# Strassen's seven products in the down projection, with the residual stream kept token-major

## The chip, the cores and the metric

One core of one Trainium2 chip. The metric is the device time of one execution in microseconds (us); the times shown are medians of several runs. Everything is computed in float32 precision: an operand is held as two float32r parts, a high part and the remainder, and a product of two operands takes three matmuls on TensorE (`mm3`: high by high, high by low, low by high).

## What is computed

One layer of a decoder trunk for 512 tokens with 1024 channels. Cut to what the change touches:

```python
x = x + (g_a * y_a + g_b * y_b) @ w_out[i]                     # 1024 x 1024
h = rmsnorm(x, ffn_norm[i])
x = x + conv_ffn(h, w_up[i], conv_w[i], conv_b[i], w_down[i])   # 1024 -> 2 * 2816, causal conv of width 3,
                                                               # gelu(a) * b, 2816 -> 1024
gate = jax.nn.sigmoid(rmsnorm(x, ple_norm[i]) @ w_ple_gate[i])  # 1024 x 1024
x = x + gate * (p[i] @ w_ple[i])                               # 256 -> 1024
return rmsnorm(x, final_norm)
```

Ahead of it stand two mixers (an input projection to five outputs of 1024 channels, pooling, spatial gating, two branch projections); the change leaves their arithmetic as it was.

## The kernel before

The work runs in stages one behind the other: input projections, mixers, branch projections, output projection (`w_out`), up projection with the convolution, down projection, and the last stage (embedding gate, embedding, final norm, output).

**Layouts.** A tile holds 128 channels by 512 tokens (channel-major) or 128 tokens by 1024 channels (token-major). Contractions need their operand channel-major. The mixer's output `ga` is token-major; `turn` (L566) turns it by 32 TensorE transposes of 128x128. From there the residual `x` is channel-major until the last stage, where `turn_back` (L688) turns it into token-major tiles `xt`, again 32 transposes. The norm before the up projection is not applied to its input: its factor, a row over tokens, is made on TensorE (`Norm.token` L257, four matmuls of one column; `Norm.row` L263, two matmuls of 512 columns) while the first up projections run, and each of the 44 up outputs is multiplied by it on VectorE (L607).

**Weights.** `plan` queues each block of weights (128x1024, 512 KB). `take` hands out the next one and keeps two more ready; `prepare` loads up to four ahead on SP's DMA queue (L77), then cuts the block in two: ScalarE makes the high part `whi` (L64), VectorE the remainder `wlo` (L65). The cut parts stand in four pairs of buffers, so a block's cut waits until TensorE is through with the block four places ahead.

**Seven products.** Three of the input projections and the embedding gate use Strassen's scheme in Winograd's form (`seven`, L312): a product of two operands, each seen as 2 by 2 blocks, from seven block products in place of eight. The sums of activation blocks are made by `combine` (L284), the sums of weight blocks on VectorE (L101) or, for the embedding gate's first two, by an accumulating DMA on POOL's queue (L96). The partial results stand in two PSUM banks `seeded` that are copied out by ScalarE (L349, L352) before the next product adds to them.

**Down projection.** `down` (L628) accumulates 22 channel tiles into each of eight outputs, 128 channels by 512 tokens: 22 x 8 x 3 = 528 matmuls of 512 columns. The operands of the embedding gate (`operands`, L640) are made while the down projection still runs for three of the four pairs of channel tiles; the fourth is made behind it.

The order of instructions on each engine is set by the tile framework when the program is built, from the order in which the code is written and from dependencies; on the chip each engine then goes through its own list in that order.

Of the kernel before, what the change touches and what calls it, by code (L numbers as in the profile page):

```python
# [32 lines left out]


# [6 lines left out]
def trunk(ctx, tc, xT, pT, wsT, par, bsp, w_u0, w_u1, w_v, w_ga, w_gb, w_p, w_pl,  # L41
# [37 lines left out]

    def plan(src, cols=CW, **kw):  # L80
        got = []
        todo.append((lambda: got.append(load_raw(src)), lambda: parts(got[0], cols, **kw)))

    def plan_seven(w, summed=False, spare=()):

        raw = {}

        def unit(load_, dst, kk, add=None):  # L90
            def load():
                if load_:
                    name, *src = load_
                    t = raw[name, kk] = load_raw(w["abdc".index(src[0]), kk])
                    for z in src[1:]:
                        G.dma_start(t, w["abdc".index(z), kk], accum_op=ALU.add)  # L96

            def cut():
                t = raw[dst, kk]
                if add:  # L100
                    V.tensor_tensor(t, t, raw[add, kk], op=ALU.add)  # L101
                return parts(t, spare=dst in spare and not add)

            todo.append((load, cut))

        for args in ((("a", "a"), "a"), (("t", "b", "a"), "t"), (("c", "c"), "t", "c"), (("s", "b", "c"), "s"),
                     (("d", "d"), "t", "d"), (None, "d"), (None, "c")) if summed else (
                     (("a", "a"), "a"), (("b", "b"), "a", "b"), (("c", "c"), "a", "c"), (None, "b", "c"),
                     (("d", "d"), "a", "d"), (None, "d"), (None, "c")):
            for kk in range(2):  # L110
                unit(args[0], args[1], kk, *args[2:])
# [18 lines left out]
    plan_seven(w_v)  # L130
    plan_seven(w_ga)
    plan_seven(w_gb)
# [11 lines left out]
    for f in range(KD):  # L144
        plan(w_o[f].rearrange(flat))
    for i in range(2 * KF):
        plan(w_up[i].rearrange(flat))
    DK = [(k0, min(8, KF - k0)) for k0 in range(0, KF, 8)]
    ORDER = [f for k in range(HK) for f in (k, HK + k)]

    def plan_down(f, k0, n):
        plan(w_dn[f, :, k0:k0 + n, :].rearrange(flat), n * P)

    for f in ORDER[:-2]:
        for k0, n in DK:
            plan_down(f, k0, n)
    for k0, n in DK:
        for f in ORDER[-2:]:
            plan_down(f, k0, n)
    for k in range(2):  # L160
        plan(w_ple[k])
    plan_seven(w_g, summed=True, spare="c")
# [123 lines left out]
    def combine(k, s1, s2, E):  # L286

        d = work("d").rearrange("p (a t) -> p a t", a=2)
        e = work("e").rearrange("p (a t) -> p a t", a=2)
        E.tensor_tensor(d[:, 0], s1[:, H:], s2[:, H:], op=ALU.subtract)  # L290
        E.tensor_tensor(d[:, 1], d[:, 0], s1[:, :H], op=ALU.subtract)
        E.tensor_tensor(e[:, 0], s1[:, :H], s1[:, H:], op=ALU.subtract)
        E.tensor_tensor(e[:, 1], s2[:, :H], d[:, 1], op=ALU.add)
        o = []
        for src in (d, e):
            t = block("cmb", (2, 2, H), F32R)
            S.copy(t[:, :, 0], src)
            V.tensor_tensor(t[:, :, 1], src, t[:, :, 0].bitcast(F32), op=ALU.subtract)
            o.append(t)
        return o  # L300

    class Operand:


        def __init__(self, whole, cmb):
            self.whole, self.cmb = whole, cmb

        def get(self, c, k, j):

            if c in ("A11", "A12", "A22"):  # L310
                t, c0 = self.whole[k + (HK if c[2] == "2" else 0)], H if c[1] == "2" else 0
            else:  # L312
                i = ("D", "S2", "S3", "E").index(c)
                t, c0 = self.cmb[k][i // 2][:, i % 2], 0
            return act(t, slice(c0 + j * P, c0 + (j + 1) * P))

    def seven(op, drain, fill=(), tail=False):

        fill = list(fill)
        ahead = AHEAD + 2 if tail else AHEAD

        def step(o, c, w, kk, first):
            for j, c0, n, t in o:
                for k2 in range(2):
                    k = 2 * kk + k2
                    mm3(t, op.get(c, k, j), [z[:, c0:c0 + n] for z in wslice(w, k2, T)], first and k == 0, k == HK - 1,
                        skip_group_check=True)

        def product(o, c, first=False):
            for kk in range(2):
                step(o, c, take(ahead), kk, first)
                if fill:
                    fill.pop(0)()

        def whole(banks):
            return [(j, 0, T, t) for j, t in enumerate(banks)]

        a, b = whole([bank() for _ in range(2)]), whole(seeded)  # L340
        product(a, "A11", first=True)
        for j in range(2):
            S.copy(seeded[j], a[j][3])
        c = [(0, 0, T, bank())] + ([(1, 0, H, bank()[:, :H]), (1, H, H, bank()[:, :H])] if tail else [(1, 0, T, bank())])
        product(c, "D", first=True)
        product(b, "S2")
        u = [[work("u") for _ in range(2)] for _ in range(2)]
        for j in range(2):
            S.copy(u[0][j], seeded[j])  # L349
        product(b, "S3")  # L350
        for j in range(2):
            S.copy(u[1][j], seeded[j])  # L352

        def minus(p, z):
            j, c0, n, t = p
            o = z[j][:, c0:c0 + n]
            V.tensor_tensor(o, t, o, op=ALU.subtract)  # L357
            return o

        for p in c:  # L360
            minus(p, u[1])
        for j in range(2):
            drain(1, j, 1, u[1][j], 0)
        product(b, "A22")
        for j in range(2):
            drain(1, j, 0, seeded[j], 0)
        product(a, "A12")
        for j, _, _, t in a:
            drain(0, j, 0, t, 0)
        if not tail:  # L370
            product(c, "E")
            for p in c:
                drain(0, p[0], 1, minus(p, u[0]), 0)
        else:
            ws = [take(ahead) for _ in range(2)]
            for p in c:
                for kk in range(2):
                    step([p], "E", ws[kk], kk, False)
                drain(0, p[0], 1, minus(p, u[0]), p[1])
        for f in fill:  # L380
            f()
# [45 lines left out]
    cmb = []  # L427
# [4 lines left out]
    for f in range(KD):  # L432
# [4 lines left out]
        if f % 2:  # L437
            k = f // 2
            s = []
            for i in (k, HK + k):  # L440
                s.append(work("sx"))
                S.activation(s[-1], x[i], AF.Copy, scale=col(C_MIX, i))
            cmb.append(combine(k, *s, V))
    X = Operand(xg, cmb)
# [40 lines left out]
    def gate(op, fill=()):  # L485
# [8 lines left out]
        seven(op, drain, fill)  # L494
# [60 lines left out]
    x2.clear()  # L555
    x.clear()
    for k in range(KD):
        if k % 2 == 0:
            x2.append(block("x"))
        x.append(x2[-1][:, k % 2])  # L560
        later(x[k][:, :1], ga[0][:, 0, :1])
        nc.scalar.dma_start(x[k], xT[k])

    m = []

    def turn(fs):  # L566

        for f in fs:
            tp = bank()
            for b in range(NT):  # L570
                PE.transpose(tp[:, b * P:(b + 1) * P], ga[b][:, f // 4, f % 4 * P:(f % 4 + 1) * P], ident)  # L571
            m.append(split(tp))

    def residual(f, o, cg, nm=None):

        V.tensor_tensor(x[f], o, x[f], op=ALU.add)
        b = split(x[f], col(cg, f))
        if nm is not None:
            nm.add(x[f])
        return b  # L580
# [10 lines left out]
    for f in range(2):  # L591
        for k in range(HK, KD):
            mm3(seeded[f], wslice(c[f], k), act(m[k]), False, k == KD - 1)
        xg.append(residual(f, seeded[f], C_FFN, nm))
    for f in range(2, KD):
        xg.append(residual(f, proj8(m), C_FFN, nm))


    up_o = [proj8(xg)]
    r_tok = nm.token()  # L600
    up_o.append(proj8(xg))
    R = nm.row(r_tok)

    def conv(i):
        o = up_o[i] if i < len(up_o) else proj8(xg)
        z = work("up")
        V.tensor_tensor(z, o, R, op=ALU.mult)  # L607
        cc = work("cc")
# [38 lines left out]

    for f in ORDER[:-2]:
        down([f])
# [167 lines left out]
```

## Time and profile before

| | |
|---|---|
| median of 3 runs | 790.32 us (790.09 to 791.33) |
| the profiled execution | 790.46 us, of which the span in the trace is 788.8 us |
| TensorE (PE) busy | 775.5 us, 98% of the span |
| VectorE (DVE) busy | 524.5 us, 67% |
| ScalarE (ACT) busy | 362.7 us, 46% |
| GpSimd (POOL) busy | 31.2 us, 4% |
| moved by DMA | 86.68 MB |

Busy shares are means over stages with different limits. Matmuls overlap: one lasts 390 ns and the next starts 227 ns behind its start, so TensorE's work is counted in starts.

### The profile page before, as it was taken

Reading aid. Unit: us, or ns where it says so; the run is one execution under the profiler, and the core shown is the slowest. Engines: PE = TensorE matmul, PEld = TensorE weight load, DVE = VectorE, ACT = ScalarE, POOL = GpSimd, SP = SyncE. Lnnn points to the kernel's source line nnn. Section 1 sums busy time; section 2 is a strip of 40 time slices with the busy share of each in tenths; the row PEclk is TensorE's granted clock in tenths of the full one; section 3 lists DMA queues with packets and bytes.
Section 4 is the critical chain, followed back from the end, with each engine's and each line's share of the span. In section 5 each row is a group of like instructions: output and inputs, shape, how many; then the busy total and the mean of one; then the engine's idle time right before and its main releaser. Section 6 shows DMA issues by size and latency. Waiting matters only on the chain.

```text
span 788.8 us, 9104 instructions
## 1 busy us (share of the span) xinstructions
PE 775.5 (98%) x3502; PEld 643.5 (82%) x3502; DVE 524.5 (67%) x713; ACT 362.7 (46%) x499; POOL 31.2 (4%) x68
## 2 busy tenths in 40 slices
PE   9999999999999999999999999999999999999994
PEld 8888878888888888888888888888888888888883
DVE  7797898865576744665877777777776234355666
ACT  6576736582142321442644444444444223244974
POOL 0000200000112100000000000000000000000201
PEclk9999999999999999999999999999999999999998
DMA  9612225134031507515221121211216430137302
GB/s 351 267 54 81 80 81 187 53 108 161 27 133 57 211 11 282 210 58 187 81 81 53 54 80 56 80 54 53 81 52 224 138 101 0 47 134 236 84 1 107
DMA packets 26683, 86.68 MB, mean 110 GB/s; under 512 B 3088, under 2 KB 3216, under 8 KB 26640
## 3 DMA queue, kind: packets, MB, share of 16 engines
q1 hardware_dynamic: 23904, 79.70, 28.5%
q10 hardware_dynamic: 2160, 4.31, 1.6%
q0 software_dynamic: 576, 2.10, 1.5%
q8 instruction: 27, 0.44, 0.2%
q14 instruction: 16, 0.13, 0.0%
HBM read 84.00 MB, written 2.10 MB: 109 GB/s over the span
## 4 chain that ended last, share of the span: by engine, by line
PE 94%; DVE 3%; ACT 1%; issue 1%; POOL 0%; POOLq 0%; ACTq 0%; DVEq 0%
PE mm L166 26%; PE mm L167 26%; PE mm L168 25%; PE sd L167 5%; PE sd L166 5%; PE sd L168 5%; PE mm L475 1%; DVE raw L101 1%; PE wake L223 1%; DVE xt L724 0%; PE mm L571 0%; DVE wlo L65 0%; DVE ple L723 0%; ACT whi L64 0%; DVE u L357 0%
## 5 line engine op out<-in xcount | busy, mean ns | idle before, releaser
L64 ACT CAST whi<-raw 128x1024 fp32r<-128x1024 f32 (+2 forms) x165 | 171.1, 1039 | 253.1 <-PE mm L167 123.0
L65 DVE TENSOR_TENSOR wlo<-raw,whi 128x1024 fp32r<-128x1024 f32 (+1 forms) x172 | 203.1, 1185 | 116.3 <-ACT whi L64 114.8
L166 PE MATMUL mm<-blk,whi 128*128 128x512 f32 x704 | 274.0, 390 | 0.0
L167 PE MATMUL mm<-blk,whi 128*128 128x512 f32 x704 | 273.9, 389 | 0.0
L168 PE MATMUL mm<-blk,wlo 128*128 128x512 f32 x704 | 273.8, 389 | 0.0
L166 PEld LDWEIGHTS mm<-blk,whi 128*128 128x128 f32 x704 | 132.4, 188 | 28.0 <-ACT blk L201 0.3
L168 PEld LDWEIGHTS mm<-blk,wlo 128*128 128x128 f32 x704 | 132.1, 188 | 27.5
L167 PEld LDWEIGHTS mm<-blk,whi 128*128 128x128 f32 x704 | 132.2, 188 | 27.3
L166 PE MATMUL mm<-whi,blk 128*128 128x512 f32 x160 | 62.7, 392 | 0.0
L167 PE MATMUL mm<-wlo,blk 128*128 128x512 f32 x160 | 62.4, 390 | 0.0
L168 PE MATMUL mm<-whi,blk 128*128 128x512 f32 x160 | 62.3, 389 | 0.0
L607 DVE TENSOR_TENSOR up<-mm,R 128x512 f32<-128x512 f32 x44 | 30.2, 687 | 38.5 <-PE mm L168 38.5
L198 ACT CAST blk<-cc 128x512 fp32r<-128x512 f32 x22 | 13.7, 621 | 57.3 <-DVE cc L621 57.3
L609 ACT ACTIVATE cc<-up,pr 128x512 f32<-128x512 f32 x44 | 35.7, 813 | 1.8 <-DVE up L607 1.6
L166 PEld LDWEIGHTS mm<-whi,blk 128*128 128x128 f32 x160 | 30.0, 188 | 6.4 <-ACT mm L696 0.2
L168 PEld LDWEIGHTS mm<-whi,blk 128*128 128x128 f32 x160 | 30.0, 188 | 6.2
L167 PEld LDWEIGHTS mm<-wlo,blk 128*128 128x128 f32 x160 | 30.1, 188 | 6.0
L612 DVE SCALAR_TENSOR_TENSOR cc<-up,pr,cc 128x510 f32<-128x510 f32 x44 | 33.0, 749 | 1.5
L101 DVE TENSOR_TENSOR raw<-raw 128x1024 f32<-128x1024 f32 x28 | 33.8, 1228 | 0.1
L610 DVE SCALAR_TENSOR_TENSOR cc<-up,pr,cc 128x511 f32<-128x511 f32 x44 | 32.8, 745 | 0.3 <-ACT cc L609 0.3
L619 ACT ACTIVATE cc<-cc 128x512 f32<-128x512 f32 x22 | 13.9, 632 | 39.1 <-DVE cc L612 39.1
L166 PE MATMUL sd<-whi,blk 128*128 128x512 f32 x80 | 31.4, 393 | 0.0
(160 smaller groups left out, 835.9 us busy)
## 6 DMA issues: line engine op xcount, KB each, us to landing
raw<-in_w_up SPq DMA_DIRECT2D x44, 512.0 KB, 3.3
raw<-in_w_dn SPq DMA_DIRECT2D x16, 512.0 KB, 3.6
raw<-in_w_g SPq DMA_DIRECT2D x10, 512.0 KB, 5.7
raw<-in_w_v SPq DMA_DIRECT2D x8, 512.0 KB, 10.5
raw<-in_w_ga SPq DMA_DIRECT2D x8, 512.0 KB, 4.2
raw<-in_w_gb SPq DMA_DIRECT2D x8, 512.0 KB, 3.5
raw<-in_w_p SPq DMA_DIRECT2D x8, 512.0 KB, 4.5
raw<-in_w_b SPq DMA_DIRECT2D x8, 512.0 KB, 3.5
```

Source lines behind the costliest of these rows:

```text
L64: (V.tensor_copy if first else S.copy)(hi[:, :cols], raw[:, :cols])
L65: V.tensor_tensor(lo[:, :cols], raw[:, :cols], hi[:, :cols].bitcast(F32), op=ALU.subtract)
L101: V.tensor_tensor(t, t, raw[add, kk], op=ALU.add)
L166: PE.matmul(o, wh, ah, start=first, stop=False, **kw)
L167: PE.matmul(o, wh, al, start=False, stop=False, **kw)
L168: PE.matmul(o, wl, ah, start=False, stop=last, **kw)
L198: S.copy(b[:, 0, :], src)
L607: V.tensor_tensor(z, o, R, op=ALU.mult)
L609: S.activation(cc, z, AF.Identity, scale=col(C_CW, 3 * i + 2), bias=col(C_CB, i))
L610: V.scalar_tensor_tensor(cc[:, 1:], z[:, :T - 1], col(C_CW, 3 * i + 1), cc[:, 1:], op0=ALU.mult, op1=ALU.add)
L612: V.scalar_tensor_tensor(cc[:, 2:], z[:, :T - 2], col(C_CW, 3 * i), cc[:, 2:], op0=ALU.mult, op1=ALU.add)
L619: S.activation(a, a, AF.Gelu)
```

## The change

1. The down projection becomes seven products (`seven`), in three parts over the hidden channels: channel tiles in pairs, eleven pairs, parts of 4, 4 and 3 pairs. A part runs in the middle of the up projection as soon as its pairs exist: behind up pair 8, behind up pair 16, and at the end. Each adds its result to `x`.
2. The sums of weight blocks for it are made by DMA alone (`adds="all"`): per chunk of weights five plain loads and four accumulating DMAs on POOL's queue, the second and third sum in the same buffer behind the first, after that one was cut.
3. `x` stays token-major from the mixer's output on: `w_out` is multiplied with the turned mixer output `m` as the stationary operand (`by_token`), the sum of squares comes from ScalarE per token, the norm is applied (`xn`, L665 of the changed kernel), and `xn` is turned by 32 transposes for the up projection. The factor on 44 up outputs, `Norm.row` and `Norm.token` of this norm go.
4. The 32 transposes of the mixer's output now all stand ahead of the output projection; before, 24 matmuls stood between two groups of them.
5. Behind the down projection `x` is turned for the gate: first the upper 256 tokens (`turn_half(1, k)`), then half of the embedding's matmuls, then the lower 256 tokens (`turn_half(0, k)`) with all the sums that need both halves. The gate's products run in another order (`LAST`: P5 first). The other half of the embedding is computed earlier, ahead of the up projection, and kept in DRAM.
6. `w_v`, `w_ga`, `w_gb`, `w_dn` and `w_g` lie in memory as blocks of 128x512, so that a load has rows of 2 KB in place of 4 KB.

```diff
+INNER = ("P1", "P5", "P6", "P7", "P4", "P2", "P3")
+DOWN = ("P1", "P5", "P2", "P6", "P7", "P4", "P3")
+LAST = ("P5", "P1", "P6", "P7", "P4", "P2", "P3")
+PARTS = ((0, 4), (4, 4), (8, 3))
...
+        def add_to(t, name, ch):
+            fetch(t, name, ch, accum_op=ALU.add)
...
+            need = {"P1": [("a", "a")], "P5": [("b", "b")] if inplace else [("t", "b", "a")],
+                    "P6": [] if adds == "all" else [("c", "c")], "P7": [] if inplace else [("s", "b", "c")],
+                    "P4": [] if adds == "all" else [("d", "d")], "P2": [("d", "d")], "P3": [("c", "c")]}[prod]
...
+                o = parts(z, cols, spare=prod in spare)
+                if adds == "all" and prod in ("P5", "P6"):
+                    add_to(z, "c" if prod == "P5" else "d", ch)
+                return o
...
-    nm = Norm()
-    xg = []
-    turn(range(HK))
-    c = [take(), take()]
-    for f in range(2):
-        for k in range(HK):
-            mm3(seeded[f], wslice(c[f], k), act(m[k]), k == 0, False)
-    turn(range(HK, KD))
...
+    for f in range(KD):
+        m.append(split(turned(ga, f)))
+    xss = [small.tile([P, 2], F32, tag="xss", name="xss", bufs=NT) for _ in range(NT)]
+    for fh in range(2):
+        banks = [bank() for _ in range(NT)] if fh == 0 else [*seeded, bank(), bank()]
+        by_token(m, fh, banks, range(KD // 2))
+        for b in range(NT):
+            V.tensor_tensor(x[b][:, fh], banks[b], x[b][:, fh], op=ALU.add)
+            squares(b, fh, xss)
...
+    for b in range(NT):
+        r = rstd_1([xss[b][:, 0:1], xss[b][:, 1:2]])
+        for fh in range(2):
+            V.tensor_scalar_mul(xn[b][:, fh], x[b][:, fh], r)
+    xg = [split(turned(xn, f), col(C_FFN, f)) for f in range(KD)]
...
+        if i % 2 == 0:
...
+            cut_into(t11[:, n11], a[:, :H])
+            first = a
+        else:
+            z = split(a)
+            hc.append(dict(A11=t11[:, n11], A12=z[:, :, :H], A22=z[:, :, H:], **combine(first, a)))
+            n11 += 1
+        part = blocks_of_down[i]
+        if part:
+            q0, n = part
+            seven(hc[q0:q0 + n], drain_x(q0 + n == KF // 2), DOWN)
...
+    for k in range(HK):
+        t1, z1 = G1[k]
+        t = turn_half(0, k)
+        V.tensor_tensor(t1[:, 3], t1[:, 2], t[:, 0], op=ALU.subtract)
+        V.tensor_tensor(t[:, 2], t[:, 0], t1[:, 0], op=ALU.subtract)
+        V.tensor_tensor(t[:, 3], t[:, 1], t1[:, 3], op=ALU.add)
...
+        cut_into(t2[:, k % 2], t1[:, 3])
+        z0, z3 = halves(t[:, 0:2], 2), halves(t[:, 2:4], 2)
```

**Where instructions now stand.** Three places of the program, with the semaphores that an instruction waits for in brackets (DMASW: an accumulating DMA of POOL's queue; DMAHW: a load of SP's queue).

ScalarE's list inside a run of `seven`, before: in the projection `w_ga`, from the copies behind the first product (`sd`) to the copies behind the third (`u`).

```order
L343 COPY sd_129<-mm_899 128x512 [waits PE_49]
L343 COPY sd_130<-mm_900 128x512 [waits PE_49]
L64 CAST whi_942<-raw_772 128x1024 [waits DVE_49]
L64 CAST whi_961<-raw_796 128x1024 [waits DVE_49]
L64 CAST whi_988<-raw_814 128x1024 [waits PE_49]
L64 CAST whi_1013<-raw_838 128x1024 [waits PE_49,Activation_49]
L64 CAST whi_1044<-raw_772 128x1024 [waits DVE_49,PE_49,Activation_49]
L349 COPY u_1037<-sd_129 128x512 [waits PE_49]
L349 COPY u_1038<-sd_130 128x512 [waits PE_49]
```

The same stretch of the changed kernel in the first part of the down projection: the cuts of P2's second chunk, of P6, of P7 and of P4's first chunk, then the copies behind P6.

```order
L402 COPY sd_129<-mm_3761 128x512 [waits PE_49]
L402 COPY sd_130<-mm_3762 128x512 [waits PE_49]
L69 CAST whi_3822<-raw_3763 128x1024 [waits DMAHW5_49]
L69 CAST whi_3841<-raw_3629 128x1024 [waits DMASW1_49,PE_49]
L69 CAST whi_3858<-raw_3686 128x1024 [waits DMASW3_49,DVE_49,PE_49]
L69 CAST whi_3877<-raw_3819 128x1024 [waits DMASW4_49,DVE_49,PE_49]
L69 CAST whi_3895<-raw_3838 128x1024 [waits DMASW5_49,DVE_49,PE_49]
L69 CAST whi_3917<-raw_3629 128x1024 [waits DMASW6_49,DVE_49,PE_49]
L372 COPY u_3911<-sd_129 128x512 [waits PE_49]
L372 COPY u_3913<-sd_130 128x512 [waits PE_49]
```

The copies that free the `seeded` banks for P7 now stand behind a cut that waits for the sixth accumulating DMA of the part.

POOL's list of accumulating DMAs in that part, of which before there was none (raw_3629 and raw_3686 are the sums of the two chunks for P5, P6 and P4, raw_3819 and raw_3838 those for P7).

```order
L106 DMA raw_3629<-in_w_dn 128x2x512 [waits DMASW0_49,DVE_49]
L106 DMA raw_3686<-in_w_dn 128x2x512 [waits DMAHW5_49,DMAHW3_49,PE_49]
L106 DMA raw_3686<-in_w_dn 128x2x512 [waits DMASW2_49,DVE_49]
L106 DMA raw_3819<-in_w_dn 128x2x512 [waits DMAHW4_49,DMAHW6_49,DMAHW0_49,PE_49]
L106 DMA raw_3838<-in_w_dn 128x2x512 [waits DMAHW7_49]
L106 DMA raw_3629<-in_w_dn 128x2x512 [waits DMASW1_49,DVE_49]
L106 DMA raw_3686<-in_w_dn 128x2x512 [waits DMASW3_49,DVE_49]
```

Seven of the part's eight stand here, the first (raw_3629, DMASW0) ahead of them. The third waits for VectorE's cut of P5's second chunk, and the two for P7 stand behind it.

VectorE's list at the start of the gate's products, before: two small norm steps, then cuts and sums of weights alone.

```order
L668 TENSOR_SCALAR fms_5544<-xss_5530 128x1 [waits Activation_49]
L670 SCALAR_TENSOR_TENSOR fms_5544<-xss_5530,fms_5544 128x1 [waits DVE_49,Activation_49]
L65 TENSOR_TENSOR wlo_5592<-raw_5396,whi_5591 128x1024 [waits DMASW0_49,Activation_49]
L101 TENSOR_TENSOR raw_5396<-raw_5396,raw_5467 128x1024 [waits DMAHW7_49,DVE_49]
L65 TENSOR_TENSOR wlo_5599<-raw_5460,whi_5598 128x1024 [waits DMASW1_49,PE_49,Activation_49]
L668 TENSOR_SCALAR fms_5657<-xss_5624 128x1 [waits Activation_49,Pool_49]
L101 TENSOR_TENSOR raw_5460<-raw_5460,raw_5589 128x1024 [waits DMAHW0_49,DVE_49]
```

Now, for the first of four k of the lower 256 tokens (xf_5630 and xf_5737 are the turned tiles of the upper and lower half, raw_5567 the weights' sum for P6).

```order
L750 TENSOR_TENSOR xf_5630<-xf_5630,xf_5737 128x256 [waits Activation_49]
L751 TENSOR_TENSOR xf_5737<-xf_5737,xf_5630 128x256
L752 TENSOR_TENSOR xf_5737<-xf_5737,xf_5630 128x256 [waits DVE_49,Activation_49]
L138 TENSOR_TENSOR raw_5567<-raw_5567,raw_5686 128x1024 [waits DMAHW7_49]
L333 TENSOR_TENSOR s2_5743<-xf_5630,s2_5743 128x256 [waits Activation_49]
L333 TENSOR_TENSOR cmb_5746<-xf_5737,cmb_5746 128x2x256 [waits Activation_49]
L333 TENSOR_TENSOR cmb_5749<-xf_5737,cmb_5749 128x2x256 [waits Activation_49]
L750 TENSOR_TENSOR xf_5642<-xf_5642,xf_5757 128x256 [waits Activation_49]
```

Sums and remainders of activations stand between the cuts of weights here, six instructions for each k.

## Rows read from the trace of the kernel before

**Rows 1.** The page's first part: busy us (share of the span) xinstructions.

```profile
PE 775.5 (98%) x3502; PEld 643.5 (82%) x3502; DVE 524.5 (67%) x713; ACT 362.7 (46%) x499; POOL 31.2 (4%) x68
```

**Rows 2.** What PE waited for, whole span: us in total, times, longest us.

```profile
PE wake L223 <- DVE neghalf L227: 1.1, 1, 1.1
PE sd L166 <- ACT u L349: 0.8, 1, 0.8
```

**Rows 3.** Busy time by stretch: us, PE, PEld, DVE, ACT, POOL (instructions), PEclk, DMA share, GB/s.

```profile
376.70:726.20 349.50, 349.50 (x1543) 289.37 (x1542) 220.27 (x283) 144.71 (x179) 1.91 (x2) 1.00 0.26 85
...
777.50:780.00 2.50, 0.05 (x1) 0.00 (x0) 2.38 (x8) 1.63 (x4) 0.18 (x1) 1.00 0.00 0
780.00:784.00 4.00, 0.00 (x0) 0.00 (x0) 3.20 (x9) 1.02 (x4) 0.55 (x2) 0.65 0.34 131
784.00:788.80 4.80, 0.00 (x0) 0.00 (x0) 0.49 (x1) 0.72 (x1) 0.47 (x1) 0.50 0.28 109
```

**Rows 4.** Timeline of PE at the norm: start us, us, instruction.

```profile
364.85 0.39 PE L168 MATMUL mm<-blk,wlo 128*128 128x512 f32 x1
...
368.25 0.39 PE L168 MATMUL mm<-blk,wlo 128*128 128x512 f32 x1
368.48 0.95 PE L260 MATMUL ss<-ones,acc 128*128 128x1 f32 x8
369.29 0.49 PE L166 MATMUL mm<-blk,whi 128*128 128x512 f32 x1
```

**Rows 5.** Timeline of PE at the mixer's transposes.

```profile
315.24 0.40 PE L168 MATMUL mm<-whi,blk 128*128 128x512 f32 x1
315.48 1.91 PE L571 MATMUL mm<-ident,sg 128*128 128x128 f32 x16
317.32 0.73 PE L166 MATMUL sd<-blk,whi 128*128 128x512 f32 x2
```

**Rows 6.** Timeline of DVE at the same place.

```profile
316.29 1.28 DVE L553 TENSOR_TENSOR sg<-sg 128x512 f32<-128x512 f32 x2
317.49 2.47 DVE L199 TENSOR_TENSOR blk<-mm,blk 128x512 fp32r<-128x512 f32 x4
```

**Rows 7.** Groups by shape on DVE and ACT: busy us, mean ns of one, idle before.

```profile
L65 DVE TENSOR_TENSOR wlo<-raw,whi 128x1024 fp32r<-128x1024 f32 x156 | 190.0, 1222 | 91.2 <-ACT whi L64 89.8
L607 DVE TENSOR_TENSOR up<-mm,R 128x512 f32<-128x512 f32 x44 | 30.2, 687 | 38.5 <-PE mm L168 38.5
L202 DVE SCALAR_TENSOR_TENSOR blk<-mm,pr,blk 128x512 fp32r<-128x512 f32 x8 | 5.9, 747 | 1.5 <-ACT blk L201 1.5
L292 DVE TENSOR_TENSOR e<-sx 128x256 f32<-128x256 f32 x8 | 3.3, 417 | 0.0
L64 ACT CAST whi<-raw 128x1024 fp32r<-128x1024 f32 x156 | 163.7, 1052 | 228.3 <-PE mm L167 99.0 <-issue 54.2 <-PE mm L168 27.9
L201 ACT ACTIVATE blk<-mm,pr 128x512 fp32r<-128x512 f32 x8 | 5.4, 687 | 2.6 <-PE mm L168 2.6
L725 ACT ACTIVATE u<-xt 128x256 f32<-128x256 f32 x2 | 0.8, 416 | 2.7 <-DVE xt L724 2.7
L349 ACT COPY u<-sd 128x512 f32<-128x512 f32 x8 | 4.6, 587 | 2.2 <-PE sd L168 2.1
```

**Rows 8.** DMA queues: packets, MB, share of 16 engines (q1 SP's, q0 the accumulating).

```profile
q1 hardware_dynamic: 23904, 79.70, 28.5%
...
q0 software_dynamic: 576, 2.10, 1.5%
```

**Rows 9.** The accumulating DMAs (L96), issue to landing; a plain load's median; two issues together.

```profile
DMA to landing us min/median/max: 5.3/6.4/9.2
raw<-in_w_up SPq DMA_DIRECT2D x44, 512.0 KB, 3.3
735.63 1.76 POOL L96 DMA_DIRECT2D raw<-in_w_g  x2
```

**Rows 10.** Busy time by stretch, two microseconds of the last stage (columns as rows 3).

```profile
738.00:740.00 2.00, 2.00 (x11) 1.65 (x10) 1.97 (x2) 1.97 (x4) 0.00 (x0) 1.00 0.94 184
```

More of the change, by code (lines that the diff above doesn't have):

```diff
@@ L82, in plan, with plan_seven @@
         todo.append((lambda: got.append(load_raw(src)), lambda: parts(got[0], cols, **kw)))
-    def plan_seven(w, summed=False, spare=()):
+    def plan_seven(w, order=INNER, adds="vector", spare=(), q0=0, n=HK):
         raw = {}
-        def unit(load_, dst, kk, add=None):
-            def load():
[L92 to L96, printed above, removed]
-            def cut():
[L99 to L102, printed above, removed]
-            todo.append((load, cut))
[L106 to L111, printed above, removed]
@@ L113, in prepare @@
+        for prod in order:
+            for ch in pairs_of(n):
+                unit(prod, ch)
     def prepare(loads=LOADS):
@@ L321, in seven @@
         fill = list(fill)
+        n = len(op)
         ahead = AHEAD + 2 if tail else AHEAD
[L324 to L328, printed above, removed]
-                        skip_group_check=True)
-        def product(o, c, first=False):
-            for kk in range(2):
-                step(o, c, take(ahead), kk, first)
+        bank_of = {}
@@ new lines, in seven, with step, copies @@
+        begun = set()
+        u = [[None, None], [None, None]]
+        def step(o, c, w, ch, first):
+            for j, c0, m, t in o:
+                for i in range(ch[1]):
+                    k = ch[0] + i
+                    a = op[k][c]
+                    a = [a[:, z, j * P:(j + 1) * P] for z in range(2)]
+                    mm3(t, a, [z[:, c0:c0 + m] for z in wslice(w, i, T)], first and k == 0, k == n - 1,
+                        skip_group_check=True)
+        def copies(i):
+            for j in range(2):
+                u[i][j] = work("u")
+                S.copy(u[i][j], seeded[j])
@@ new lines, in minus @@
+        def minus(p, z):
+            j, c0, m, t = p
+            o = z[j][:, c0:c0 + m]
+            V.tensor_tensor(o, t, o, op=ALU.subtract)
+            return o
+        for prod in order:
+            b, c = ops[prod]
+            if b not in bank_of:
+                bank_of[b] = [(j, 0, T, seeded[j] if b == "b" else bank()) for j in range(2 if b != "c" or not tail else 1)]
+                if b == "c" and tail:
+                    bank_of[b] += [(1, 0, H, bank()[:, :H]), (1, H, H, bank()[:, :H])]
+            o = bank_of[b]
+            first = b != "b" and b not in begun
+            begun.add(b)
+            if prod == "P3" and tail:
+                ws = [take(ahead) for _ in pairs_of(n)]
+                for p in o:
+                    for w, ch in zip(ws, pairs_of(n)):
+                        step([p], c, w, ch, False)
+                    drain(0, p[0], 1, minus(p, u[0]), p[1])
+                continue
+            for ch in pairs_of(n):
+                step(o, c, take(ahead), ch, first)
@@ L334, in product @@
                 if fill:
                     fill.pop(0)()
[L337 to L346, printed above, removed]
@@ L364, in seven @@
[L364 to L379, printed above, removed]
+            if prod == "P1":
+                for j in range(2):
+                    S.copy(seeded[j], o[j][3])
+            elif prod == "P6":
+                copies(0)
+            elif prod == "P7":
+                copies(1)
+                for p in bank_of["c"]:
+                    minus(p, u[1])
+                for j in range(2):
+                    drain(1, j, 1, u[1][j], 0)
+            elif prod == "P4":
+                for j in range(2):
+                    drain(1, j, 0, seeded[j], 0)
+            elif prod == "P2":
+                for p in o:
+                    drain(0, p[0], 0, p[3], 0)
+            elif prod == "P3":
+                for p in o:
+                    drain(0, p[0], 1, minus(p, u[0]), 0)
@@ L595, in trunk @@
[L595 to L608, printed above, removed]
-        S.activation(cc, z, AF.Identity, scale=col(C_CW, 3 * i + 2), bias=col(C_CB, i))
-        V.scalar_tensor_tensor(cc[:, 1:], z[:, :T - 1], col(C_CW, 3 * i + 1), cc[:, 1:],
-                               op0=ALU.mult, op1=ALU.add)
-        V.scalar_tensor_tensor(cc[:, 2:], z[:, :T - 2], col(C_CW, 3 * i), cc[:, 2:],
-                               op0=ALU.mult, op1=ALU.add)
-        return cc
@@ L640, in operands @@
[L640 to L652 removed]
+    x = [block("x") for _ in range(NT)]
+    for b in range(NT):
+        later(x[b][:, 0, :1], ga[0][:, 0, :1])
+        nc.scalar.dma_start(x[b].rearrange("p a t -> p (a t)"), xr[b])
@@ L673, in rstd_1, with squares, columns, turned @@
         return r
-    ple = [None] * NT
-    xt = [None] * NT
-    xss = [None] * NT
-    r_emb = [None] * NT
+    def squares(b, fh, sums):
+        sq = work("sq")
+        S.activation(sq, x[b][:, fh], AF.Square, accum_out=sums[b][:, fh:fh + 1])
+    def columns(z, b, f):
+        return z[b][:, f // HK, f % HK * P:(f % HK + 1) * P]
+    def turned(z, f):
+        tp = bank()
+        for b in range(NT):
+            PE.transpose(tp[:, b * P:(b + 1) * P], columns(z, b, f), ident)
+        return tp
```

304 lines of the change are left out of this document (154 added, 150 removed).

## The prediction, made before the changed kernel ran

> **What bounds the kernel now.** I read the busy times first: TensorE is busy for 98% of the span, VectorE for 67%, ScalarE for 46% [rows 1]. Then the list of what TensorE waited for: 1.9 us in all, of which 1.1 is the start [rows 2]. So the other engines are hidden everywhere: less work on them gains nothing, less work on TensorE gains its whole time, and every wait that the change puts on TensorE is paid in full. The question is whether the new order keeps TensorE as well fed.
>
> The unit is the step from one 512-column matmul's start to the next: 15 steps from 364.85 to 368.25 us, 0.227 each [rows 4].
>
> **What TensorE no longer does.** Seven products instead of eight: 11 channel pairs x 7 products x 2 token tiles x 3 = 462 matmuls, where 528 stood: 66 fewer. With the two matmuls of the norm's row 68 x 0.227 = 15.4 us. The four one-column matmuls of the norm took 369.29 - 368.48 = 0.8, and the next matmul came some 0.1 late [rows 4]. Together **16.3 us**. The 44 multiplications by the norm's factor (30.2 us of VectorE [rows 7]) count nothing, since they are hidden: VectorE was busy for 220 of 349 us in that stretch [rows 3].
>
> **What TensorE does in addition.** 32 transposes (xn). Sixteen took 317.32 - 315.48 = 1.84 us, 0.115 each [rows 5]: **3.7 us**. The transposes for the gate and the embedding only move. TensorE's work falls by 12.6 us.
>
> **Waits that the change adds.** I follow the lists of instructions by hand, with the durations of the rows.
>
> *Mixer output to output projection.* The last branch matmul ended at 315.64 [rows 5], VectorE's last sum at 317.57, and the remainders of the turned tiles then followed every 0.62 us [rows 6]. Before, 24 matmuls stood between the two groups of transposes; now the fifth to eighth tile wait for that sum and for one of five PSUM banks, and the projection's first bank is the one that the fourth remainder frees, at 317.57 + 4 x 0.62 = 320.05. That is 4.4 us with 3.7 us of transposes: **1.0** with hand-overs. Bounds: 0 and 2.
>
> *Norm.* Behind the last matmul come the residual sum, squares on ScalarE, four small steps, POOL's power and the scaling, some 6 us; 24 matmuls of the embedding cover 5.4. Then the transposes, and the first up projection needs the banks of the fourth and fifth tile back, whose remainders take VectorE 0.75 each [rows 7]: it starts 10.3 us behind the last matmul with 9.0 us of work done. **1.4**; bounds 0.5 and 3.
>
> *Parts of the down projection.* This is a matter of DMA. A plain load of 512 KB costs 28.5% of 788.8 us x 0.524/79.70 = 1.48 us of all engines, an accumulating one 1.5% of 788.8 / 4 = 2.96 [rows 8]. A part of four pairs needs ten plain and eight accumulating ones, 14.8 + 23.7 = 38.5 us, beside 168 x 0.227 = 38.1 us of matmuls. Seven of the eight must run between the cut for P5 and the copies behind P6, for each waits for the last: the lists show ScalarE's copies that free the banks for P7 behind a cut that needs the sixth, and the third on POOL behind P5's second cut, with the two for P7 behind it. P5's first cut ends 3 us before the part starts (its buffer comes free with the last but one up projection). The next two DMAs land 6 to 7 us after that; the chunk is cut by 7 to 9, the third starts then, and three more follow at 3 us each. The sixth lands at 21.5 to 23.5, the cut takes 1.05 and the copy 0.59 [rows 7], so P7 starts at 23 to 25 where it could at 21.8; plain loads in between add up to 3 us. I take **3.5** for each of the two large parts. In the last part (three pairs, smaller second chunk, only one copy behind that cut) I find **1.5**; its last operand comes in time, since P1 and the first chunk of P5 cover the chain. Sum 8.5. Bounds: 1, if the plain loads are all early and the engine shares better than one behind the other; 18, if rows of 2 KB make the accumulating ones slower by a third.
>
> For the accumulating transfer the rows say 6.4 us from issue to landing, and 5.3 at the least [rows 9]. The Trainium skill, "DMA: Bandwidth & Descriptors", section "Anatomy of one DMA — SWDGE (gpsimd) path", gives 2.0 us plus the bytes over 436 GB/s for a transfer from that queue: an estimate of 3.2 us for 512 KB; by it the waits of the two large parts would go and the sum be 7 us lower. Here the trace disagrees: two issued together [rows 9] kept the engines at 0.94 with 184 GB/s [rows 10]. I take the rows.
>
> *Last stage.* Before, three of four operand pairs of the gate were made under the down projection. Now all are made behind it. VectorE's work from the end of P3 to the cut for P7's second chunk, by its list: 13 passes over weights at 1.14, 16 of 512 columns at 0.61, 20 of 256 at 0.34 (the durations of [rows 6, 7], less the 0.08 by which neighbours overlap), and 1.1 of small ones: 32.5 us. TensorE's work to the same point: two groups of transposes 3.7, embedding 24 x 0.227 = 5.4, P5 5.6, P1 and P6 5.4 each, half of P7 2.7: 28.2. So at least 4.3 us of waiting, without any hand-over. It will not run that smoothly. For each of four k of the upper half ScalarE scales two turned tiles (256 columns, 0.45 each; [rows 7] has 0.42 for another form), VectorE subtracts (0.42), ScalarE casts (0.62): 1.95 a round, behind 2.2 us of residual sums; then a cut of weights and four copies out of PSUM stand on ScalarE before P5 gets its first bank, at 14 us, where TensorE has 9 us of work: 5. P1's bank waits for the third tile of the lower half, some 2, its right-hand operands another 2, P6 1 and P7's cut 2. I take **11**; bounds 4.3 and 15. Before, VectorE was already busy for 1.97 of 2 us there with weights alone [rows 10], which speaks for the upper half.
>
> The end (the last matmuls, drains, output) is the same code. The start is the same.
>
> **Sum.** 790.5 (the profiled execution, 0.1 above the median) - 16.3 + 3.7 + 1.0 + 1.4 + 8.5 + 11 = 799.8; against the median 799.7. I say **799**: slower.
>
> **Rivals.**
>
> *Throughput decides, not hand-over (the other side).* If the lists run ahead of TensorE as well as before, where a VectorE busy for 1.97 of 2 us held up nothing [rows 2, 10], only what the engines' work forces is left: 1 and 0.5 at the turns, 2.5 in the parts, 4.3 in the last stage, 8.3 in place of 21.9: 786.2. It decides the sign where the waits stay under 12.6 us in all. Against it: the copies behind an accumulating transfer are a dependency and no matter of throughput.
>
> *Accumulating transfers bound the parts.* Each costs a third more with rows of 2 KB, 3.9 us: a large part then needs 14.8 + 31.5 = 46 us of DMA for 38 of matmuls. Two parts lose 8 each and the last 3 in place of 8.5: 810. For it: the engines stood at 0.94 with 184 GB/s [rows 10]. Against: half the rate comes from reading the target, which does not depend on the row's length.
>
> *The clock.* After the last matmul at 777.5 the granted clock was 1.00 until 780, 0.65 from 780 to 784 and 0.50 from there [rows 3], so it fell some 4 us behind the last matmul to the lower level, 1.2 GHz. A wait of that length in the last stage could do it in the middle: P5 and P1 at half the rate cost up to 11 us more: 811. Against: transposes and matmuls of the embedding fall into the wait before P5. The Trainium skill, "TensorE: Matmul & The Clock Gate", section "HAM oscillation — how this bites in real kernels", names this as what waits inside a matmul stage cost; by that rule the last stage would be paid twice. The trace agrees that the clock falls when TensorE idles, and shows no case inside the kernel.
>
> **Chances.** Forecast 0.55, throughput 0.25, transfers 0.12, clock 0.08. The range 785 to 812 takes in the bounds of the parts (1 to 18 in place of 8.5) and of the last stage one at a time, and both ends' rivals; both at their lower bounds give 785.6, at their upper ones 813.3. My own case alone gives 793 to 806. About 0.2% is what a measurement of this kernel can tell. Faster by more: 0.24, nearly all from the throughput case; within: 0.08, the edge between it and mine; slower: 0.68.
>
> **What would show it.** Right: TensorE's 512-column matmuls number 3224 where 3292 stood, at 0.227 us; its list of waits names ScalarE's copies of `sd` to `u` behind P6 (some 3 us in each large part), the scaling and the copies out of PSUM in the last stage, and VectorE's sums before the second group of the mixer's transposes. VectorE is busy almost without a break for the first 40 us of the last stage. Wrong: fewer than 12.6 us of waits on TensorE; or waits that are long but stand elsewhere, as at the loads of the up weights, since SP's queue shares the DMA engines; or a granted clock under 1.00 inside the span.

## The result and the profile after

The change takes **808.27 us** (median of 4 runs, 806.84 to 809.77) where the kernel before takes 790.6 beside it: ratio 1.0223, 95% interval 1.0202 to 1.0244. I had forecast 799, so slower was right and the loss is twice the forecast one: +17.7 us, not +8.7. The profiled execution took 809.77 us, span 808.1, 19.3 more than that of before. One of all the runs in this document, of the last experiment (970.71 us, granted clock 0.751 in the mean), was in a slow state and is left out of its time.

The page, its rows on busy time, the two load queues and the loads of the feed-forward weights:

```profile
PE 773.3 (96%) x3458; PEld 635.6 (79%) x3458; DVE 553.9 (69%) x783; ACT 389.6 (48%) x566; POOL 60.5 (7%) x95
...
q1 hardware_dynamic: 33760, 85.73, 30.3%
q0 software_dynamic: 7104, 13.63, 10.0%
...
raw<-in_w_dn POOLq DMA_DIRECT2D x20, 512.0 KB, 7.8
```

Against [rows 1], TensorE's busy time fell by 2 us only, though the 512-column matmuls number 3224 where 3292 stood and the work shrank by 12.6: something ran slower. The half clock shown below is 5.5 us of the missing 10.4; the rest are the ends and restarts of matmuls around the new waits, in which the engine counts as busy. The accumulating transfers cost 10.0% of 808.1 us for 13.63 MB (26 times 512 KB), 3.11 us per 512 KB, where [rows 8] gave 2.96. That 2.96 hangs on a share rounded to 1.5%: from 690 to 760 us of the trace before, where all four of its transfers stand, the queue's row is

```profile
q0 software_dynamic: 576, 2.10, 17.4%
```

and 17.4% of 70 us over four is 3.05. From issue to landing the 20 of the down projection in the last row took 7.8 us (median), not the 6.4 of [rows 9].

What TensorE waited for, the first rows (us in total, times, the longest):

```profile
PE sd L205 <- ACT u L372: 12.8, 5, 5.4
PE mm L205 <- ACT xf L727: 3.0, 3, 1.3
PE mm L724 <- ACT ple L652: 1.3, 1, 1.3
```

The waits stand where the prediction put them: behind P6 of the parts, and in the last stage. The first row is 12.8 us, with one wait over 5 us in each large part. Windows of TensorE around these two waits (busy, count, granted clock, DMA share, GB/s):

```profile
496.00:500.00 4.00, 0.00 (x0) 0.92 1.12 216
500.00:504.00 4.00, 3.61 (x9) 0.50 1.05 367
504.00:508.00 4.00, 4.00 (x15) 0.73 0.80 299
508.00:512.00 4.00, 4.00 (x19) 1.00 0.54 154
...
628.00:632.00 4.00, 0.52 (x3) 1.00 1.13 206
632.00:636.00 4.00, 2.08 (x5) 0.56 1.06 338
636.00:640.00 4.00, 4.00 (x12) 0.59 0.74 289
640.00:644.00 4.00, 4.00 (x19) 1.00 0.55 189
```

The clock fell to 0.50 (1.2 GHz in place of 2.4) before each wait was over, and stayed there for some 5.5 us of matmuls behind it, one every 0.427 us: TensorE counts as busy and does half the work.

To see the whole difference I summed, over the starts of all matmuls, what each step is longer than 0.227 us (0.115 for transposes and 256 columns). From each stretch I took off what it had in excess in the kernel before. Work -12.6; mixer's turn +2.0 (1.0 of it listed as waits); norm +0.9; waits in the parts, with their restarts, +13.9; steps at half clock behind them +2.7 and +2.8; last stage +9.0 (10.0, where before had 1.0); from the last matmul to the end +1.0 (12.5 us, before 11.5); the start -0.4. Sum +19.3, measured 19.3. A single trace bears these terms to about 1 us: the turn's excess, 2.3 us in this one, was 1.0 to 1.2 in six of the nine runs below, which have the same code there.

ScalarE before the wait in the first part shows its cause (the last row is TensorE's, P7's first matmul):

```profile
493.71 1.05 ACT L69 CAST whi<-raw 128x1024 fp32r<-128x1024 f32 x1 [3.13 <-DMA raw<-in_w_dn]
496.26 1.04 ACT L69 CAST whi<-raw 128x1024 fp32r<-128x1024 f32 x1 [1.50 <-DMA raw<-in_w_dn]
498.81 1.04 ACT L69 CAST whi<-raw 128x1024 fp32r<-128x1024 f32 x1 [1.50 <-DMA raw<-in_w_dn]
499.76 1.07 ACT L372 COPY u<-sd 128x512 f32<-128x512 f32 x2
500.39 0.79 PE L205 MATMUL sd<-whi,cmb 128*128 128x512 f32 x1 [5.07 <-ACT u L372]
```

P6's last matmul started at 494.93. The two copies out of its banks, for which P7 waits, stand behind three cuts that each wait for a transfer: both chunks for P7, then the first for P4, which nobody needs before P7 is done.

### The profile page after: what moved, and what is told of

It reads as the page before. It is cut to its first block, busy times and chain, and to the rows that moved or that the text cites. A ratio compares the mean times of both kernels' runs of the same rounds, so it can differ in the third digit from the quotient of the medians.

```text
span 808.1 us, 9316 instructions
## 1 busy us (share of the span) xinstructions
PE 773.3 (96%) x3458; PEld 635.6 (79%) x3458; DVE 553.9 (69%) x783; ACT 389.6 (48%) x566; POOL 60.5 (7%) x95
## 3 DMA queue, kind: packets, MB, share of 16 engines
q0 software_dynamic: 7104, 13.63, 10.0%
## 4 chain that ended last, share of the span: by engine, by line
PE 47%; issue 27%; DMA 11%; DVE 8%; ACT 5%; POOL 1%; POOLq 0%; SPq 0%; ACTq 0%; DVEq 0%
PE mm L205 10%; PE mm L206 10%; PE mm L207 10%; DMA raw<-in_w_dn 9%; PE sd L205 6%; PE sd L206 6%; PE sd L207 6%; DVE wlo L70 2%; ACT whi L69 2%; DMA pt<-in_pT 1%; DVE raw L138 1%; POOL raw L106 1%; PE mm L514 1%; DVE x L773 0%; DVE ple L784 0%
## 5 line engine op out<-in xcount | busy, mean ns | idle before, releaser
L69 ACT CAST whi<-raw 128x1024 fp32r<-128x1024 f32 (+1 forms) x185 | 189.8, 1032 | 232.4 <-PE mm L206 56.2
L206 PE MATMUL mm<-blk,whi 128*128 128x512 f32 x480 | 186.8, 389 | 0.0
L205 PE MATMUL mm<-blk,whi 128*128 128x512 f32 x480 | 186.4, 390 | 0.3 <-ACT blk L240 0.3
L207 PE MATMUL mm<-blk,wlo 128*128 128x512 f32 x480 | 186.6, 389 | 0.0
L205 PEld LDWEIGHTS mm<-blk,whi 128*128 128x128 f32 x480 | 90.0, 188 | 19.6 <-ACT blk L240 0.9
L206 PEld LDWEIGHTS mm<-blk,whi 128*128 128x128 f32 x480 | 90.1, 188 | 18.8
L207 PEld LDWEIGHTS mm<-blk,wlo 128*128 128x128 f32 x480 | 90.1, 188 | 18.6
L205 PE MATMUL mm<-whi,blk 128*128 128x512 f32 x214 | 83.9, 392 | 1.2 <-ACT xf L727 1.2
L207 PE MATMUL mm<-whi,blk 128*128 128x512 f32 x214 | 83.3, 389 | 0.0
L205 PE MATMUL sd<-whi,cmb 128*128 128x512 f32 x108 | 45.5, 421 | 12.8 <-ACT u L372 12.3
L205 PE MATMUL mm<-whi,cmb 128*128 128x512 f32 (+1 forms) x132 | 50.1, 380 | 2.1 <-ACT xf L727 1.8
L206 PE MATMUL mm<-wlo,cmb 128*128 128x512 f32 (+1 forms) x132 | 49.8, 377 | 0.4 <-DVE wlo L70 0.4
L207 PE MATMUL mm<-whi,cmb 128*128 128x512 f32 (+1 forms) x132 | 49.3, 376 | 0.0
L206 PE MATMUL sd<-wlo,cmb 128*128 128x512 f32 x108 | 44.3, 410 | 0.3 <-DVE wlo L70 0.3
L207 PE MATMUL sd<-whi,cmb 128*128 128x512 f32 x108 | 43.9, 408 | 0.0
```

The costliest lines, as they stand in the source:

```text
L69: (V.tensor_copy if first else S.copy)(hi[:, :cols], raw[:, :cols])
L205: PE.matmul(o, wh, ah, start=first, stop=False, **kw)
L206: PE.matmul(o, wh, al, start=False, stop=False, **kw)
L207: PE.matmul(o, wl, ah, start=False, stop=last, **kw)
```

## The experiments

**copies_first** pins one cut in each part: in ScalarE's order in the two large parts only this cast moves, from ahead of the two copies to behind them.

```diff
-                o = parts(z, cols, spare=prod in spare)
+                o = parts(z, cols, spare=prod in spare, keep=adds == "all" and prod == "P4" and ch[0] == 0)
```

with `tc.keep_in_program_order(cast)` in `parts` where `keep` is set.

> The change with one ScalarE instruction moved in each part: the cut of P4's first chunk of weights, which waits for an accumulating transfer, stands behind the two copies u<-sd of P6 and not ahead of them. Transfers and everything else are as they were. Theory A (the wait before P7 is the copies standing behind that cut, and the fallen clock follows from the wait): P7 starts as soon as its own weights are cut, some 0.8 us after P6; of the 5.1 + 5.4 + 1.1 us of waits about 2 stay, the granted clock stays at 1.00, which gives back another 5.5: about 794 us. Theory B (the transfers themselves are too slow, at a DMA share of 1.0): the wait moves to P4, whose weights come when they came before; P7 is done 4 us earlier and PE idles there instead, so the sum of waits falls by less than 3 us and the clock may fall still: 803 to 808.

Measured: 802.8 us, ratio 1.0146 (1.0131 to 1.0161). By its number this lies beside theory B's range. The trace says otherwise: the wait still named the copies (2.4 and 3.3 us), now behind the cut for P7's own second chunk:

```profile
494.10 1.04 ACT L69 CAST whi<-raw 128x1024 fp32r<-128x1024 f32 x1 [1.51 <-DMA raw<-in_w_dn]
495.05 1.07 ACT L374 COPY u<-sd 128x512 f32<-128x512 f32 x2
```

The clock fell behind each of the two, and a third time in the last stage (TensorE busy, count, granted clock, DMA share, GB/s):

```profile
496.00:500.00 4.00, 4.00 (x12) 0.57 1.09 279
740.00:744.00 4.00, 2.37 (x12) 0.79 0.36 135
744.00:748.00 4.00, 4.00 (x21) 0.78 0.74 226
```

So the run did not decide. **copies_all** carries the edit on: `keep` also for P4's second chunk and P7's second, and one chunk less is prepared ahead at the end of P6 and P7.

```diff
-                step(o, c, take(ahead), ch, first)
+                short = order is DOWN and prod in ("P6", "P7") and ch[0] > 0
+                step(o, c, take(ahead - 1 if short else ahead), ch, first)
```

> copies_first carried on: ScalarE's copies of P6 and of P7 now stand ahead of every cut that is not needed before them (P7's second chunk and both of P4), all transfers kept. copies_first still waited 2.4 and 3.3 us at P7, now behind the cut of P7's second chunk, and the clock fell once more behind each. If the order on ScalarE is the cause and the transfers come in time by themselves: P7 starts 0.6 us behind P6, P4's second chunk waits 1.4 us in each large part, no fall of the clock: 795 to 796. If the transfers are the bound by now: the wait stands in the middle of P7 and before P4, 3 us or more in each part, and the clock falls: 800 to 803.

Measured: 795.09 us, 1.0057 (1.0042 to 1.0072), and the copies are all but gone from the waits:

```profile
PE mm L208 <- ACT xf L731: 3.2, 4, 1.3
PE sd L208 <- ACT whi L69: 1.3, 2, 0.8
PE mm L728 <- ACT ple L656: 1.3, 1, 1.3
PE sd L208 <- ACT u L375: 1.1, 2, 0.8
```

All 28 accumulating transfers (24 of 512 KB, four of half that) are still there. The order on ScalarE, with the one chunk less prepared ahead and the half clock in it, was worth 13.2 of the 17.7 us.

**vector_sums** takes the accumulating transfers out of the down projection (24, four of them of half size): `plan_seven(blocks(w_dn), DOWN, "vector", ...)` in place of `"all"`.

> The change with the sums of the down projection's weights made by VectorE (eight passes over two chunks of 1024 columns in a part of four pairs, about 9 us of VectorE at 1.14 us each) and no accumulating transfer there; the 20 of the down projection are gone. Theory A: no cut waits long for a transfer, so the waits in the parts fall from 12.8 us to what the same products show in the mixer (0.8 us each), VectorE at about 55% has room for 9 us in 38, the clock stays at 1.00: 790 to 793 us. Theory B gives the same here, since the load on the DMA engines falls too. A third, that VectorE becomes the bound inside the parts: waits on wlo or raw of some 3 us in each part: 796 to 800.

Measured: 790.29 us, 0.9993 (0.9983 to 1.0002). In both large parts TensorE had no gap, and VectorE, busy for 31.6 of 38.1 us there (the row's third pair), held up nothing, so the third theory falls:

```profile
471.83:509.91 38.08, 38.08 (x169) 31.54 (x168) 31.64 (x34) 18.84 (x23) 0.00 (x0) 1.00 0.53 194
```

That is 4.8 us under copies_all: so much the transfers still cost with the order put right, by the traces 4.2 in the parts and 0.7 at the end. **some_sums** (`"some"`: half of those transfers kept):

> The change with half of the sums of the down projection's weights on VectorE: P5 and P7 keep their accumulating transfers (four in a part of four pairs), the sums for P6 and P4 are VectorE's (four passes of 1024 columns). If the length of the chain of transfers on one buffer (a added, cut, c added, cut, d added) makes the wait, it is gone as in vector_sums: 790 to 792. If what counts is only how many accumulating transfers a part has, half of the waits stay and the clock falls behind some of them: 796 to 800.

Measured: 791.07 us, 1.0006 (0.9996 to 1.0015). Four accumulating transfers in a part that stand in no chain are 0.8 us from none, which the two intervals don't tell apart, so the count alone is not what hurt. The copies behind P6 still stand behind as many cuts as in the change: the order costs only where a cut comes late. Whether the chain on one buffer makes the cuts late, or the load on the DMA engines (four transfers fewer in a part, 4 x 3.1 = 12 us of all engines by my estimate), this run does not separate.

**warm** leaves the waits and fills them.

```diff
             elif prod == "P6":
                 copies(0)
+                if order is DOWN and n == 4:
+                    dm = pst.tile([P, T], F32, tag="st", name="dm")
+                    for _ in range(40):
+                        tc.keep_in_program_order(PE.matmul(dm[:, :H], ones_r, op[0]["A11"][:, 0, :], start=True, stop=True))
```

> The change with 40 matmuls of 256 columns whose result nobody reads, put on TensorE between P6 and P7 of the two large parts, where it waits 5.1 and 5.4 us; they take about 4.6 us at full clock. If the clock falls because TensorE idles there, it stays at 1.00 and the 2.7 and 2.8 us that the half clock costs behind each wait are won, the waits themselves being as long as before in sum: 803 us. If something else takes the clock (the DMA load, or a power limit that more matmuls would only sharpen): 808 to 809, with the clock at 0.5 as before.

Measured: 803.18 us, 1.0151 (1.0128 to 1.0174), 5.1 less than the change, with 80 matmuls more. Around the first wait:

```profile
492.00:496.00 4.00, 4.00 (x31) 1.00 1.14 208
496.00:500.00 4.00, 3.22 (x23) 1.00 1.09 255
500.00:504.00 4.00, 4.00 (x20) 1.00 1.01 406
```

P7 started 5.6 us behind P6 (5.2 in the change), at full clock and under the same DMA load. So the idle time took the clock, not the load. In the second part P7 started 4.8 us behind P6 (5.6 in the change) and the four runs spread from 800.86 to 804.83, so the 5.1 us are no exact price of the clock; the steps at half clock give 5.5.

**early_turn** asks what bounds the last stage: `turn_half(1, k)` with its split moves from behind the last part to between P4 and P3.

> The change with the turning and splitting of the upper half of the tokens for the gate moved ahead of P3 of the last part (they need only what P7 and P4 leave). My theory of the last stage (VectorE and ScalarE have 32 us of work in a chain where TensorE has 28, all of it behind P3): some 7 us of it lie beside P3 now, the waits of the last stage fall from about 10 us to 5: 803 us. The rival (the stage is bound by the lower half's chain, which still begins behind P3's sums): the waits before the embedding's end go, those behind it stay, 2 to 3 us are won: 805 to 806. Clock and waits in the parts as in the change.

Measured: 819.31 us, 1.0348 (1.0321 to 1.0374): a clear miss, 11 us slower than the change. POOL and ScalarE show why:

```profile
749.33 1.20 POOL L106 DMA_DIRECT2D raw<-in_w_g  x1
...
750.02 0.51 ACT L696 ACTIVATE xf<-mm,pr 128x256 f32<-128x256 f32 x1
759.02 1.04 ACT L69 CAST whi<-raw 128x1024 fp32r<-128x1024 f32 x1 [8.48 <-DMA raw<-in_w_g]
759.97 0.47 ACT L696 ACTIVATE xf<-mm,pr 128x256 f32<-128x256 f32 x1
```

The transfer for P5's second chunk was issued at 749.3, behind four power operations of the last norm (in the change both of P5's at 718.6). The cut that waits for it stood between two halves of one turned tile; TensorE waited 7.2 us and the clock fell to 0.50. It is the parts' pattern over again, and says nothing of VectorE. **vector_turn_keep** puts it right: vector_sums, the early turn, and `tc.keep_in_program_order` on the four powers of `r_emb`.

> vector_sums with the upper half turned ahead of P3 of the last part, as in early_turn, and the four small power operations of the last norm pinned on POOL behind the accumulating transfer for P5's second chunk, which early_turn's order had put behind them. Theory: early_turn lost its 11 us because that transfer was issued late (749.3 instead of 720) and the cut that waits for it stood ahead of ScalarE's scaling of the turned tiles; with the transfer early, the wait of 7.2 us goes and the early turning wins: waits of the last stage 5 in place of 10 us, 785 us. Rival: the buffer that the transfer needs comes free only with P3, so the cut stays late and ScalarE behind it: 790 or more.

Measured: 789.19 us, 0.9982 (0.9973 to 0.9992). The long wait is gone, but only 1.1 us are won on vector_sums. One wait of 1.9 us was left, at P1, and the clock fell behind it:

```profile
736.00:740.00 4.00, 2.13 (x15) 1.85 (x15) 3.86 (x10) 3.24 (x7) 1.19 (x1) 1.00 0.89 310
740.00:744.00 4.00, 4.00 (x12) 3.02 (x11) 4.00 (x10) 2.95 (x7) 1.20 (x1) 0.57 1.02 234
```

(Busy and count of TensorE, its weight loads, VectorE, ScalarE and POOL, then granted clock, DMA share, GB/s.) **best** moves two instructions more on ScalarE: the cut for P6's first chunk gets a manual dependency on the last scaling of the fourth turned tile, and the load of `gB` is gated on that tile's sums and not on `x[3]`.

> vector_turn_keep with two instructions moved in the last stage: the cut of P6's first chunk stands on ScalarE behind the scaling of the fourth turned tile of the lower half (it had stood ahead of it, waiting for TensorE, while P1 waited 1.9 us for the bank that the scaling frees, and the clock fell to 0.57 behind that wait), and ScalarE's issue of the load of the last norm's factors, which waited for VectorE ahead of the copies of the embedding (1.1 us on TensorE), comes later. Theory (in-order ScalarE again): about 1.5 and 1.0 us of waits and 2.3 us of clock are won, less 0.5 to 1 that P6's first cut now comes late: 785 us. Rival (VectorE, busy for 3.9 of every 4 us from 732 on, is the bound of the stage whatever ScalarE does): the waits move behind P1 and 788 to 789 stays.

Measured: 788.04 us, 0.9966 (0.9952 to 0.9979): faster than both kernels, 20 us under the change. The clock stayed at 1.00, but the time is the rival's, not 785:

```profile
736.00:740.00 4.00, 2.17 (x9) 1.26 (x8) 4.00 (x9) 3.22 (x9) 1.19 (x1) 1.00 0.93 313
740.00:744.00 4.00, 3.69 (x16) 3.03 (x17) 4.00 (x11) 2.81 (x5) 1.20 (x1) 1.00 1.06 252
```

VectorE is busy for all of these 8 us and two of TensorE's waits now name its remainders (1.3 us). **best_pool** was to relieve it: two of its three kinds of small sums for the lower half go to POOL (`V.` becomes `G.`).

> best with eight of VectorE's twelve small sums of the lower half (256 columns, 0.34 us each, 2.7 us in all) made by POOL. Theory: VectorE, busy for 3.9 to 4 of every 4 us between 732 and 744, is what bounds the last stage now, so 1.5 to 2.7 us are won there: 786. Rival: the sums are slower on POOL, and the right-hand operands of P7 and P3, and the transfers for P7's weights that stand behind them on POOL, come later: 788 or more.

Measured: 792.74 us, 1.0029 (1.0018 to 1.0040), 4.7 slower than best:

```profile
738.13 0.90 POOL L761 TENSOR_TENSOR xf<-xf 128x256 f32<-128x256 f32 x1 [1.10 <-ACT xf L703]
740.06 1.59 POOL L762 TENSOR_TENSOR xf<-xf 128x256 f32<-128x256 f32 x1 [1.03 <-DVE xf L760]
...
749.71 2.43 POOL L111 DMA_DIRECT2D raw<-in_w_g  x2
```

A sum took POOL 0.9 to 1.7 us (VectorE 0.41 each), and P7's transfers came behind them and the four powers at 749.7, where best had them at 738.3 and 740.5; P7 then waited 2.5 us, and the clock fell twice (0.59 in the mean from 744 to 748, 0.69 from 756 to 760). Whether a VectorE with less to do would shorten the stage stays open.

## Why the prediction had the sign and half the size

- **TensorE's work** (-12.6): as forecast. The matmul count is the one given, and the step stayed at 0.227 us wherever the clock was 1.00.
- **Turn and norm** (1.0 and 1.4): 2.0, of which 1.0 are listed waits and the rest restarts beside them, and 0.9: 2.9 for 2.4. That the sum comes so near is in part luck: the first is twice what I had, the second two thirds.
- **Last stage** (11, bounds 4.3 to 15): 9.0 more than before, on the releasers named: the scaling, the copies out of PSUM, the cut before P7. My five terms (5, 2, 2, 1 and 2, which add up to 12 and not to 11) came out at 4.1, 1.6, 1.4, 0.7 and 1.6, the first in three waits ahead of P5 rather than one at it. VectorE was busy for 35.7 of the stage's first 40 us, not almost without a break. Its waits were short (at most 1.3 us) and the clock stayed at 1.00, so the clock rival, which I had placed here, did not come true here.
- **Parts of the down projection** (8.5): this step failed, in the size of the waits and in what they take along. The mechanism stood as written, the copies behind a cut that needs the sixth of the seven transfers listed. But I had P7 starting 23 to 25 us into a part, and 3.5 us behind P6 with the plain loads. The first part's first matmul started at 472.73; P6 ended at 495.16, 22.4 into the part (P5 had waited 0.6), and P7 started at 500.39, 27.7 into it. I had the third of the seven start at 7 to 9 us and the sixth land 14.5 later, at 3 us for each of the four with some 2.5 of plain loads between. The third was issued at 481.88, 9.2 into the part, and the cut behind the sixth began at 498.81: 16.9 us for four. The queues' rows for this stretch:

```profile
q0 software_dynamic: 1159, 2.24, 76.3%
q1 hardware_dynamic: 294, 1.07, 17.2%
```

The accumulating transfers took 12.9 us of all engines where I had 12, the plain loads 2.9, and 1.1 of the 16.9 us went to neither. So every piece came out at the upper end of mine or above it: the two large waits were 5.2 and 5.6 us with the restart, not 3.5, and the last part's 2.4, not 1.5. The sum of waits was 13.9 with the 0.6 at P5.
- **The clock** was left out of that step. I had read in [rows 3] that it falls some 4 us behind the last matmul and kept it for the last stage at a chance of 0.08; for the waits of 3.5 us in the parts I put it at nothing, without a reason. At 5.1 and 5.4 us it fell, and in copies_first it fell behind 2.4 us, so a forecast of 3.5 should have paid for it as well. It cost 5.5 us (warm: 5.1), and with it came one of the signs that I had named for being wrong, a granted clock under 1.00 inside the span. Together, 19.4 in place of 8.5. That is all of the error: +10.9, with +1.0 at the end, +0.5 on turn and norm, -2.0 in the last stage and -0.4 at the start. What the end's 1.0 us is was not tried; it is there (12.5 to 12.7 us) in all five kernels with 28 accumulating transfers, and 11.7 to 12.0 in the changed kernels with 4 or 16. The Trainium skill, "TensorE: Matmul & The Clock Gate", section "HAM oscillation — how this bites in real kernels", describes waits inside a matmul stage behind which the next matmuls run at the lower clock; the trace agrees, at 2.7 and 2.8 us on top of the two waits.
- **Rivals.** Accumulating transfers with rows of 2 KB are about 2% dearer (3.11 against 3.05), not a third: that rival's cause is wrong, and that its 810 came near is luck. The throughput case was never run as I put it; vector_sums, which takes the transfers and not only the dependencies out of the parts, comes nearest: 790.3, not the 786.2 I gave it, since the last stage kept its 10 us.
- **Sharing of the engines.** The estimate of 3.2 us that the Trainium skill's "DMA: Bandwidth & Descriptors", section "Anatomy of one DMA — SWDGE (gpsimd) path", gives for a transfer misses the trace here too: the median from issue to landing was 7.8 us under load.

## What to carry to other kernels

Look, on an engine that works in order, at what a short instruction that frees a bank stands behind: a cut that waits for a DMA and that nobody needs yet can cost more than the DMA. Count a wait of TensorE like those here (1.9 to 5.6 us) with the half clock behind it, 1.6 to 2.8 us more in these traces, and where it can't be removed, fill it with matmuls. Sums that a transfer makes for nothing on the engines are not free where the DMA engines are busy for nine tenths of the time (0.90 from 472.73 to 512 us in the change) and sums wait for the ones before; VectorE with room made the same sums without holding TensorE up.

## What the chip did that I had not expected

The clock fell behind shorter idling than I took from [rows 3]. A wait of 2.4 us in copies_first was followed by a granted clock of 0.57 over the next 4 us, and one of 1.9 us in vector_turn_keep likewise; one of 1.4 us in best was not. But the length of one wait does not decide it. In the last stage three waits of 1.2, 0.9 and 1.3 us stand within 6 us of each other; behind the third of them the clock fell in copies_first (its rows from 740 to 748 above), and behind the same three it stayed at 1.00 in the change, copies_all, vector_sums, some_sums and warm. What tells these runs apart stays open.

In the change, the cost behind a wait (2.7 and 2.8 us) was nearly the same for 5.1 and 5.4 us of waiting; behind the waits of 2.4 and 1.9 us it was some 1.6. And forty matmuls that compute nothing, put into each wait, made the kernel 5 us faster.
